# Gates ahead of attention, tap products on ScalarE, 2048-wide low parts and 54 fused pairs in a hybrid encoder layer

## The chip, the core and the metric

The kernel runs on one core of a Trainium2 chip. TensorE (PE in the profile) multiplies matrices into PSUM, VectorE (DVE) and ScalarE (ACT) work element by element, GpSimd (POOL) and SyncE (SP) issue DMAs here. Each engine works through its own instructions in the order in which the program issued them and waits on semaphores where an operand or a buffer isn't ready. The metric is the time of one execution on the device in microseconds, the median of several.

## What is computed

One mixer layer on x of 256 rows by 4096 columns:

```python
xn = rms_norm(x, norm_g[l])
h = jnp.einsum('bsd,de->bse', xn, w_in[l])            # 4096 x 14336
c_val, c_glu, c_gate, q, k, v, a_gate = jnp.split(h, split_pts, axis=-1)
conv_out = conformer_conv(c_val, c_glu, ...)          # GLU, 31 taps, LayerNorm, swish
conv_out = conv_out * jax.nn.silu(c_gate)
q = rms_norm(q..., q_norm_g[l]); k = rms_norm(k..., k_norm_g[l])
attn = longnet_mixture(q, k, v, rel_bias)             # 16 heads of 128
attn_out = attn * jax.nn.silu(a_gate)
mixed = jnp.concatenate([conv_out, attn_out], axis=-1)
x = x + jnp.einsum('bse,ed->bsd', mixed, w_out[l])    # 4096 x 4096
```

Everything is float32. The two large products read 302 MB of weights once.

## The kernel before

**Groups and pairs.** The output columns of both products are cut into 18 groups of 1024 (`GROUPS`, L46 to L52): 14 for `w_in` (four "conv", then "agv" and "qk" four times in turn, then two "gate"), and four "out" for `w_out`. Within a group the 4096 rows of the weights come as 16 pairs of two 128-row blocks, one pair being one DMA of 1 MB into a `raw` tile (L216, three buffers, on SP's queue). `ORDERS` (L58) gives the order of the pairs in an out group; a place in it is called a slot here.

**Splitting.** Each float32 operand is split into a high part that PE reads in one pass (`fp32r`) and a low part, the difference. A product is then three matmuls: high by high, low by high, high by low (`triple`, L895). For the weights ScalarE casts the high part (L830, L860, L875) and DVE subtracts (L831, L861, L876). A plain pair has 24 matmuls of 512 columns (2 blocks of k, 2 column halves e, 2 row halves s, 3 products).

**Fused pairs.** 40 of the 288 pairs (`FUSED`, L57) are multiplied as 2 x 2 blocks with seven products in place of eight (Winograd's form of Strassen's scheme): 21 matmuls. For that the weights' blocks need sums: `split_fused` (L848) has four steps. `one` splits blocks b11 and b21 and adds two sums over them (L869), `two` splits b22 (L876), `three` splits t1 and t3 (t13h, t13l) and makes two more sums (L883, L884), `four` splits t2 and t4 (t24h, t24l). Every sum is written over the raw tile, and the cast in the next step reads it. The sums on the side of x or of the mixer's output are made once (`block_sums`, L288).

**Buffers and the order of work.** The program issues matmuls slot by slot; ahead of each triple `before` (L901) issues as many steps of the splits as have room. Room is counted in tiles of 1024 columns: 8 (`ws`) and in groups from the first fused one on 4 more out of the pool `c4` (`W_MORE`). Steps come off one queue (`todo`) strictly in the order of the pairs, and DVE and ScalarE run them in that order. What else there is to do (the convolution's taps, normalisations, attention heads, splits of the mixer's output) are generators in lanes; `pump` (L666) advances them between matmuls as far as a budget allows: each engine gets `FILL` times the matmuls' nominal 227 ns, and every step books a planned cost.

**What lies around it.** The conv taps run on DVE, one per channel block (L447, 480 instructions). The conv tile is turned channel-first with DVE transposes and 64 ScalarE copies (L418); gates, q, k and the probabilities go through DRAM on POOL's queue for this (L360). Heads run only behind group 6 (`state["side"]`, L566), when PSUM's second half is free of fused sums. The two gate groups are the last input groups; their turned tiles wait for LayerNorm (L512), and the mixer's output is split (L631) before the out groups may read it.

Of the kernel before, what the change touches and what calls it, by code (L numbers as in the profile page):

```python
# [17 lines left out]
P = 128  # L18
# [17 lines left out]
FILL, SAVED = (0.93, 0.93), (700, 700)  # L36
# [3 lines left out]
C4 = 18  # L40
# [25 lines left out]
def _relative():  # L66
# [20 lines left out]
    return bucket, pattern  # L87

# [30 lines left out]
def layer_kernel(  # L119
# [12 lines left out]

    const = ctx.enter_context(tc.tile_pool(name="const", bufs=1))
# [12 lines left out]
    def side(name):  # L146
        return ps.tile([P, 512], F32, tag="side", bufs=4, name=name)
# [4 lines left out]
    def rsqrt(src, shape, mul, eps, name):  # L152

        n = int(np.prod(shape[1:]))
        tag = "rs_small" if n <= 32 else "rs_big"
        v = sb.tile(shape, F32, tag=tag, bufs=6, name=name + "v")
        r = sb.tile(shape, F32, tag=tag, bufs=6, name=name + "r")
        t = sb.tile(shape, F32, tag=tag, bufs=6, name=name + "t")
# [12 lines left out]
        return r  # L171
# [33 lines left out]
    def load_pair(j, cuts=(0, 2048), between=None):  # L205

# [54 lines left out]
    def split_xn(k):  # L261
# [12 lines left out]
        if k % 2 and k // 2 in FUSED[FUSED_IN[0]]:  # L274
            yield from block_sums(k // 2, src_of=xT, parts=(xh, xl), out=xsum, name="xs")

    split_gens = []
# [40 lines left out]
    state = {"side": False}  # L318

# [36 lines left out]

    aT, cT, mixA = {}, {}, {}
    conv_ready = {}

    def through_dram(ways, n, name):  # L360


        ds = []
        for i, (src, _) in enumerate(ways):
            ds.append(tc.dram_tile([P, 4 * n], F32, name=f"{name}d{i}"))
            nc.gpsimd.dma_start(ds[i], src)
        yield from landing()
        for d, (_, dst) in zip(ds, ways):
            for b in range(4):
# [7 lines left out]
                )  # L377
        yield from landing()

    def turn_far(tiles, name):  # L380
# [3 lines left out]
        ways = []  # L384
        for i, tile_ in enumerate(tiles):
            tmp = t4(f"{name}{i}").rearrange("p a b -> p (a b)")
            src = tile_.rearrange("p a b -> p (a b)")
            view = tmp.rearrange("p (b t s i) -> p s t b i", b=4, t=4, s=2)
            for s in range(2):
                nc.vector.transpose(  # L390
                    view[:, s],
                    src[:, 512 * s : 512 * s + 512].rearrange("p (t b x) -> p t b x", t=4, b=4),
                )
                yield 700
            ways.append((tmp, src))
        yield from through_dram(ways, 256, name)

    def turned(tile_):

        flat = tile_.rearrange("p a b -> p (a b)")  # L400
        v = flat.rearrange("p (a t s i) -> p t s a i", a=4, t=4, s=2)
        return [v[:, t] for t in range(4)]

    def turn(tile_, name):


        tmp = t4(name)
        src = tile_.rearrange("p a b -> p (a b)")
        flat = tmp.rearrange("p a b -> p (a b)")
        for s in range(2):  # L410
            nc.vector.transpose(flat[:, 512 * s : 512 * s + 512], src[:, 512 * s : 512 * s + 512])
            yield 700
        blocks = flat.rearrange("p (s t b x) -> p s t b x", s=2, t=4, b=4)
        dst = src.rearrange("p (t s a x) -> p s t a x", t=4, s=2, a=4)
        for b in range(4):
            for a in range(4):
                v = blocks[32 * a : 32 * a + 32, :, :, b, :]
                nc.scalar.copy(dst[32 * b : 32 * b + 32, :, :, a, :], v)  # L418
            yield 0, 1610

    def glu_post(cb, a):
        yield
        yield from turn(a, f"turn_a{cb}")
        aT[cb] = a
        conv_ready[cb] = True

    def conv_gen(cb):
        while cb not in conv_ready:
            yield
        a = aT[cb]  # L430
        c = cT[cb] = t4(f"cT{cb}")
        for tp in range(0, 4, 2):
            for t in (tp, tp + 1):
                ch = 4 * cb + t
                nc.vector.tensor_scalar(
                    c[:, t, :], a[:, t, :], wT[:, ch, MID : MID + 1], col("conv_b", ch),
                    op0=ALU.mult, op1=ALU.add,
                )
                yield 410
            for k in range(TAPS):  # L440
                sh = k - MID
                if sh == 0:
                    continue
                lo, hi = max(0, -sh), min(S, S - sh)
                for t in (tp, tp + 1):
                    ch = 4 * cb + t
                    nc.vector.scalar_tensor_tensor(  # L447
                        c[:, t, lo:hi], a[:, t, lo + sh : hi + sh], wT[:, ch, k : k + 1],
                        c[:, t, lo:hi], op0=ALU.mult, op1=ALU.add,
                    )  # L450
                    yield 470

# [3 lines left out]
    def channel_mean(srcs, name, tot=None):  # L456
# [12 lines left out]
        yield  # L469
        pm = side(name + "pm")  # L470
# [4 lines left out]
    conv_done = {}  # L475

    def ln_gen():
        pm = yield from channel_mean([cT[cb] for cb in range(4)], "mu")
        mu = sb.tile([P, S], F32, tag="rs_big", bufs=6, name="mu")
# [15 lines left out]
        for cb in range(4):  # L495
# [9 lines left out]
            conv_done[cb] = True  # L505

    mix_ready = {}

    def gate_post(cb, g):
        yield  # L510
        yield from turn_far([g], f"turn_g{cb}")
        while cb not in conv_done:  # L512
            yield
        for t in range(4):
            c = by_block(cT[cb][:, t, :])
            nc.vector.tensor_mul(c, c, turned(g)[t])
            mix_ready[NH + 4 * cb + t] = c
            yield 415
# [9 lines left out]
    def qk_norm(hg):  # L528
        st = sb.tile([P, 16], F32, tag="rs_small", bufs=6, name=f"ssqk{hg}")
        both = (qt[hg], kt[hg])  # L530
        for i, src in enumerate(both):
            v = src.rearrange("p a b -> p (a b)")
            for n in range(8):
                junk = sb.tile([P, DH], F32, tag="junk", bufs=2, name=f"sq{hg}_{i}_{n}")
# [7 lines left out]
        for i, src in enumerate(both):  # L542
# [9 lines left out]
        near = t4(f"near_q{hg}")  # L552
        far = qt[hg].rearrange("p a b -> p (a b)")
        nc.scalar.activation(
            near.rearrange("p t (s a i) -> p (t s) a i", s=2, a=4),
            far.rearrange("p (a t s i) -> p (t s) a i", a=4, t=4, s=2),
            AF.Copy, scale=gqk,
        )
        qt[hg] = near
# [3 lines left out]
    def head_gen(hg, hh):  # L563
        h = 4 * hg + hh
        hs = slice(DH * hh, DH * hh + DH)
        while hg not in qk_ready or not state["side"]:  # L566
            yield
        T = sb.tile([P, 384], F32, tag="toep", bufs=3, name=f"T{h}")
# [8 lines left out]
        yield from landing()  # L577
        psc = side(f"psc{h}").rearrange("p (i j) -> p i j", i=2)
# [583 lines left out]
```

## Time and profile before

| | |
|---|---|
| median of 3 runs | 1593.95 us (1593.34 to 1594.03) |
| the profiled execution | 1593.31 us, of which the span is 1591.5 us |
| plain / fused pairs | 248 / 40 |
| ScalarE casts of plain high parts (L830) | 511.4 us, 1050 ns each |
| DVE plain low parts (L831) | 598.3 us, 1221 ns each |
| DVE conv taps (L447) | 202.8 us, 469 ns each |
| DMA | 353 MB, mean 222 GB/s |

The span runs from the first to the last instruction; the execution's own time is 1.8 us longer. The profile counts an engine as busy while an instruction is in work. Matmuls are pipelined, so that PE looks busy for 389 ns per matmul while one starts every 227 ns; the count of matmuls in a stretch is the measure of its pace. A row of a timeline gives start, duration, engine, line, operation and operands, and in brackets how long the engine had been idle and what ended the wait. DVE instructions of one row with "x2" run one into the other, so that two take less than twice one.

### The profile page before, as it was taken

To read this page: it belongs to the slowest core of one execution; us is meant where nothing else is said; L and a number is where in the kernel's file an instruction comes from. 1 tells how busy PE (TensorE), PEld (TensorE's weight loads), DVE (VectorE), ACT (ScalarE), POOL (GpSimd) and SP (SyncE) were. 2 spreads that over 40 slices of the span, in tenths; PEclk is the share of its full clock that TensorE was granted. 3 is DMA by queue.
4 is the path that set the end of the run, shared out by engine and by line. 5 is a ranking of instruction groups with operands and counts; after the bars stand their busy time and mean duration, and the time that the engine had idled before them with its cause. 6 is when DMAs were issued, how large, how long until landed. Compare 5 with 4: busy or idle time off the path is not lost.

```text
span 1591.5 us, 19107 instructions
## 1 busy us (share of the span) xinstructions
PE 1580.2 (99%) x6946; PEld 1303.2 (82%) x6946; DVE 1271.8 (80%) x1752; ACT 859.4 (54%) x1250; POOL 88.2 (6%) x164
## 2 busy tenths in 40 slices
PE   9999999999999999999999999999999999999999
PEld 8888878888888888888888888888878888888887
DVE  6669888888889888788877887887767677888887
ACT  6765555464644563546453646356576544544453
POOL 0000000000000001111121010101030200000000
PEclk9999999999999999999999999999999999999999
DMA  9867454564756366576766575755765856466653
GB/s 380 290 207 272 171 226 185 196 228 159 262 187 238 134 262 211 203 233 218 253 211 224 200 253 185 245 207 212 234 219 196 265 207 254 187 237 238 233 213 136
DMA packets 63182, 353.05 MB, mean 222 GB/s; under 512 B 8784, under 2 KB 11600, under 8 KB 26480
## 3 DMA queue, kind: packets, MB, share of 16 engines
q1 hardware_dynamic: 54096, 326.38, 56.7%
q0 software_dynamic: 8704, 25.18, 5.4%
q8 instruction: 54, 0.88, 0.2%
q10 hardware_dynamic: 288, 0.28, 0.1%
q14 instruction: 40, 0.33, 0.1%
HBM read 334.99 MB, written 16.81 MB: 221 GB/s over the span
## 4 chain that ended last, share of the span: by engine, by line
PE 86%; DVE 8%; ACT 3%; issue 2%; DMA 1%; ACTq 0%; DVEq 0%
PE acc L775 16%; PE acc L776 16%; PE acc L778 16%; PE c L898 11%; PE c L897 10%; PE c L896 10%; DVE wl L831 2%; PE m L898 1%; PE m L897 1%; PE m L896 1%; DVE t13l L861 1%; DVE raw L869 1%; DVE bl L861 1%; ACT t24h L860 1%; ACT t13h L860 1%
## 5 line engine op out<-in xcount | busy, mean ns | idle before, releaser
L831 DVE TENSOR_TENSOR wl<-raw,wh 128x1024 fp32r<-128x1024 f32 x495 | 598.3, 1221 | 214.2 <-ACT wh L830 213.4
L830 ACT CAST wh<-raw 128x1024 fp32r<-128x1024 f32 x495 | 511.4, 1050 | 379.8 <-PE acc L776 204.6
L775 PE MATMUL acc<-wh,nh 128*128 128x512 f32 x896 | 355.1, 396 | 3.9 <-ACT wh L830 3.8
L776 PE MATMUL acc<-wh,nl 128*128 128x512 f32 x896 | 349.1, 390 | 0.0
L778 PE MATMUL acc<-wl,nh 128*128 128x512 f32 x896 | 242.0, 389 | 0.0
L447 DVE SCALAR_TENSOR_TENSOR cT<-conv,wT,cT 128x241 f32<-128x241 f32 (+14 forms) x480 | 202.8, 469 | 0.0
L775 PEld LDWEIGHTS acc<-wh,nh 128*128 128x128 f32 x896 | 168.3, 188 | 40.8 <-ACT wh L830 6.0
L778 PEld LDWEIGHTS acc<-wl,nh 128*128 128x128 f32 x896 | 168.2, 188 | 35.4
L776 PEld LDWEIGHTS acc<-wh,nl 128*128 128x128 f32 x896 | 168.2, 188 | 34.9
L897 PE MATMUL c<-wh,nl 128*128 128x512 f32 x480 | 186.7, 389 | 0.0
L898 PE MATMUL c<-wl,nh 128*128 128x512 f32 x480 | 186.7, 389 | 0.0
L896 PE MATMUL c<-wh,nh 128*128 128x512 f32 x480 | 186.7, 389 | 0.0
L898 PE MATMUL c<-wl,mh 128*128 128x512 f32 x352 | 137.3, 390 | 0.1
L896 PE MATMUL c<-wh,mh 128*128 128x512 f32 x352 | 137.2, 390 | 0.0
L897 PE MATMUL c<-wh,ml 128*128 128x512 f32 x352 | 137.0, 389 | 0.0
L897 PEld LDWEIGHTS c<-wh,nl 128*128 128x128 f32 x480 | 90.1, 188 | 18.8
L896 PEld LDWEIGHTS c<-wh,nh 128*128 128x128 f32 x480 | 90.1, 188 | 18.8
L898 PEld LDWEIGHTS c<-wl,nh 128*128 128x128 f32 x480 | 90.1, 188 | 18.5
L860 ACT CAST t24h<-raw 128x1024 fp32r<-128x1024 f32 x40 | 42.0, 1050 | 112.0 <-DVE raw L884 112.0
L775 PE MATMUL acc<-wh,xh 128*128 128x512 f32 x256 | 99.8, 390 | 0.0
L776 PE MATMUL acc<-wh,xl 128*128 128x512 f32 x256 | 99.7, 390 | 0.0
L860 ACT CAST t13h<-raw 128x1024 fp32r<-128x1024 f32 x40 | 42.1, 1051 | 105.1 <-DVE raw L869 102.4
(313 smaller groups left out, 1903.6 us busy)
## 6 DMA issues: line engine op xcount, KB each, us to landing
raw<-in_w_dram SPq DMA_DIRECT2D x286, 1024.0 KB, 4.9
xT<-in_x_cols_dram SPq DMA_DIRECT2D x15, 512.0 KB, 6.7
x<-in_x_dram SPq DMA_DIRECT2D x8, 512.0 KB, 8.4
xr<-in_x_dram SPq DMA_DIRECT2D x8, 512.0 KB, 6.3
out_dram<-xr SPq DMA_DIRECT2D x15, 256.0 KB, 7.2
T<-bias_dram SPq DMA_DIRECT2D x16, 192.0 KB, 5.0
raw<-in_w_dram SPq DMA_DIRECT2D x3, 512.0 KB, 6.1
turn_qk0d<-turn_qk POOLq DMA_DIRECT2D x2, 512.0 KB, 3.6
```

The lines of the kernel that those rows point to most:

```text
L447: nc.vector.scalar_tensor_tensor(c[:, t, lo:hi], a[:, t, lo + sh : hi + sh], wT[:, ch, k : k + 1], c[:, t, lo:hi], op0=ALU.mult, op1=ALU.add,)
L775: nc.tensor.matmul(a, hs, wp, start=k == 0, stop=False)
L776: nc.tensor.matmul(a, ls, wp, start=False, stop=False)
L778: nc.tensor.matmul(a, hs, wp, start=False, stop=k == KT - 1)
L830: nc.scalar.copy(h, src)
L831: nc.vector.tensor_sub(l, src, h.bitcast(F32))
L860: nc.scalar.copy(h, src)
L861: nc.vector.tensor_sub(l, src, h.bitcast(F32))
L869: nc.vector.tensor_add(r[:, 0:2, :], r[:, 0:2, :], r[:, 1:4:2, :])
L896: nc.tensor.matmul(acc, a[0], b[0], start=start, stop=False)
L897: nc.tensor.matmul(acc, a[1], b[0], start=False, stop=False)
L898: nc.tensor.matmul(acc, a[0], b[1], start=False, stop=stop)
```

## The change

- Order: the two gate groups come directly after the four conv groups; q and k ahead of gate and v in each head group. Gates and conv tiles are turned on DVE, stored in DRAM on POOL's queue and fetched when they are needed (`to_dram`, `from_dram`); the 64 ScalarE copies go.
- Taps: in groups with fused pairs a tap's products over four channel blocks run on ScalarE into one tile `cp`, and DVE adds it in one 1024-wide instruction; in groups without, DVE may also run a tap as before (`conv_products`, `conv_gen`).
- Splits: from the third group on a plain pair has one high and one low tile of 2048 columns; the low part is one subtraction. `ws` is 4 tiles of 2048. The 4 extra tiles of `c4` hold only parts of fused pairs, from two slots ahead of the group's first fused pair. PE runs a plain pair's matmuls with the high part first, then those with the low part.
- Fused pairs: five (slots 2, 4, 6, 8, 10) in six input groups, three in the first out group (slots 12 to 14) and seven in the other three: slots 2, 4, 6, 7, 9, 10 and 12. That makes 54. The blocks of fused weights are laid out in another order by the host; the b22 split now comes ahead of the first sums, which are one wide instruction in step `two`.
- All groups from the third on run through `Stream.group`; evacuation of groups without fused pairs is on ScalarE alone. The planner's `FILL` for DVE is 0.96 in place of 0.93, lanes are cut otherwise.

```diff
-FILL, SAVED = (0.93, 0.93), (700, 700)
+FILL, SAVED = (0.96, 0.93), (700, 700)
-C4 = 18
+C4 = 17
+GROUPS += [("gate", gp, C_GATE + 1024 * gp, C_GATE + 1024 * gp + 512) for gp in range(2)]
 for _hg in range(4):
+    GROUPS.append(("qk", _hg, C_Q + 512 * _hg, C_K + 512 * _hg))
     GROUPS.append(("agv", _hg, C_AG + 512 * _hg, C_V + 512 * _hg))
-    GROUPS.append(("qk", _hg, C_Q + 512 * _hg, C_K + 512 * _hg))
-GROUPS += [("gate", gp, C_GATE + 1024 * gp, C_GATE + 1024 * gp + 512) for gp in range(2)]
...
-FUSED_IN = range(2, 7)
-FUSED = [(2, 4, 6, 8) if g in FUSED_IN else () for g in range(N_IN)] + [range(2)] + 3 * [range(6)]
+FUSED_IN = range(2, 8)
+FUSED = [(2, 4, 6, 8, 10) if g in FUSED_IN else () for g in range(N_IN)]
+FUSED += [range(3)] + 3 * [range(7)]
-ORDERS += [(8, 9, 10, 11, 6, 7, 2, 3, 0, 12, 1, 13, 14, 4, 5, 15)]
-ORDERS += 3 * [(8, 9, 0, 10, 1, 11, 2, 6, 3, 7, 4, 12, 5, 13, 14, 15)]
-W_SLOTS, W_MORE = 8, 4
+ORDERS += [(3, 4, 5, 8, 9, 10, 11, 12, 13, 14, 15, 6, 0, 1, 2, 7)]
+ORDERS += 3 * [(8, 9, 0, 10, 1, 11, 2, 3, 12, 4, 5, 13, 6, 14, 15, 7)]
+W_SLOTS, W_MORE = 4, 4
...
+    def conv_products(cb):
...
+                nc.scalar.activation(
+                    cp[:, t, lo:hi], a[:, t, lo + sh : hi + sh], AF.Copy,
+                    scale=wT[:, 4 * cb + t, k : k + 1],
+                )
+                if t == 3:
+                    made.append((k, now[0] + 1500))
...
+            if made and made[0][1] <= now[0]:
...
+                nc.vector.tensor_add(c[:, :, lo:hi], c[:, :, lo:hi], cp[:, :, lo:hi])
...
+        def room(self, n, more):
+            held = self.held
+            return held["ws"] + n <= W_SLOTS and held["c4"] + more <= self.more
...
+        def split_plain(self, u):
+            def high():
+                h = self.tile(f"wh{u}", (u, "h"), "ws")
+                for k in range(2):
+                    nc.scalar.copy(h[:, 1024 * k : 1024 * k + 1024], raw_tiles[u][:, k])
...
+            def low():
+                h, l = self.parts[(u, "h")], self.tile(f"wl{u}", (u, "l"), "ws")
+                src = raw_tiles[u].rearrange("p k c -> p (k c)")
+                nc.vector.tensor_sub(l, src, h.bitcast(F32))
...
+            return [(ONE, high), (ONE, low)]
...
             def one():
-                r = blocks()
-                both("b", r[:, 0:3:2, :], ("b11", "b21"))
-                nc.vector.tensor_add(r[:, 0:2, :], r[:, 0:2, :], r[:, 1:4:2, :])
+                both("b", blocks()[:, 0:2, :], ("b11", "b21"))
             def two():
                 r = blocks()
...
+                nc.scalar.copy(h, r[:, 2, :])
+                nc.vector.tensor_sub(l, r[:, 2, :], h.bitcast(F32))
+                nc.vector.tensor_add(r[:, 0:4:3, :], r[:, 0:3:2, :], twice(r[:, 3, :]))
             def three():
+                both("t13", blocks()[:, 0:4:3, :], ("t1", "t3"))
                 r = blocks()
+                nc.vector.tensor_add(r[:, 2, :], r[:, 0, :], r[:, 2, :])
+                nc.vector.tensor_add(r[:, 1, :], r[:, 2, :], r[:, 1, :])
             def four():
-                both("t24", blocks()[:, 0:2, :], ("t2", "t4"))
+                both("t42", blocks()[:, 1:3, :], ("t4", "t2"))
...
+                self.more = W_MORE if firsts and slot + 2 >= firsts[0] else 0
...
+            for part in "hl":
                 for e in range(2):
                     self.before()
+                    for k, (a, b) in enumerate(self.blocks_of(u, j, rows, part)):
...
+                del self.parts[(u, part)]
+                self.free((u, part))
+            pump()
```

More of the change, by code (lines that the diff above doesn't have):

```diff
@@ L274, in split_xn, with run @@
         if k % 2 and k // 2 in FUSED[FUSED_IN[0]]:
-            yield from block_sums(k // 2, src_of=xT, parts=(xh, xl), out=xsum, name="xs")
-    split_gens = []
+            sums = block_sums(k // 2, src_of=xT, parts=(xh, xl), out=xsum, name="xs")
+            if k < KT // 2:
+                yield from sums
+            else:
+                late_sums.append(sums)
+    split_gens, late_sums = [], deque()
+    def run(gen):
+        for cost in gen:
+            spend(*(cost if isinstance(cost, tuple) else (cost or 0,)))
     def split_more():
@@ L402, in turned @@
         return [v[:, t] for t in range(4)]
[L404 to L419, printed above, removed]
+    a_dram = {}
@@ L815, in step @@
         def step(self):
[L817 removed]
+            if not self.todo or not any(self.room(*need) for need in self.todo[0][0]):
                 return False
@@ new lines, in plain, with plain_last @@
+                    credit((8 if part == "h" else 4) * PRODUCT)
+                    if part == "h":
+                        pump()
+                del self.parts[(u, part)]
+                self.free((u, part))
+            pump()
+        def plain_last(self, u, j, rows, s, e, one):
+            acc = one[f"c{s + 1}{e + 1}"]
+            for part in "hl":
+                for k, (a, b) in enumerate(self.blocks_of(u, j, rows, part)):
+                    end = part == "l" and k == 1
+                    nc.tensor.matmul(acc, a[s][0], b[e], start=False, stop=end)
+                    if part == "h":
+                        nc.tensor.matmul(acc, a[s][1], b[e], start=False, stop=False)
+            credit(6 * PRODUCT)
```

397 lines of the change are left out of this document (242 added, 155 removed).

## The prediction

> **What bounds the kernel now.** I read the busy shares, then the matmul count over a long stretch, then stretches of one column group each, then the waits of PE, then the timelines of DVE and PE through one out group.
>
> ```profile
> span 1591.5 us, 19107 instructions
> PE 1580.2 (99%) x6946; PEld 1303.2 (82%) x6946; DVE 1271.8 (80%) x1752; ACT 859.4 (54%) x1250; POOL 88.2 (6%) x164
> PE 86%; DVE 8%; ACT 3%; issue 2%; DMA 1%; ACTq 0%; DVEq 0%
> 300.00:1100.00 800.00, 800.00 (x3531) 1.00 0.62 215
> 180.20:264.50 84.30, 82.43 (x358) 66.59 (x357) 72.76 (x91) 47.21 (x63) 0.00 (x0) 1.00 0.56 210
> 200.00:230.00 30.00, 28.70 (x124) 1.00 0.48 180
> 264.50:348.80 84.30, 84.30 (x374) 69.82 (x373) 72.64 (x93) 46.51 (x60) 0.00 (x0) 1.00 0.53 196
> 1163.00:1249.40 86.40, 82.47 (x358) 66.65 (x357) 61.76 (x107) 59.60 (x99) 16.44 (x30) 1.00 0.71 233
> PE m L898 <- DVE t24l L861: 2.3, 6, 0.5
> PE acc L775 <- ACT wh L830: 3.8, 4, 1.4
> ```
>
> From 300 to 1100 us PE never pauses: 800/3531 = 0.2266 us per matmul, at granted clock 1.00. All 6946 at that pace are 1573.7 us, so 17.8 us of the span is loss. It sits at the ends of the run, in the first fused group (358 matmuls where the next one has 374; between 200 and 230 us 124 where 30/0.2266 + 2 = 134 would stand, 2.2 us), in the last input group (1163 to 1249: 358 where 86.4/0.2266 = 381 would fit, 5.2 us) and in short waits for t24l. A plain pair is 24 matmuls, 5.44 us; a fused pair 21, 4.76 us. PE is the bound on average; the chain's 8% of DVE says that somewhere DVE takes over. That place is the fused stretch. One cycle of an out group, a fused pair and a plain pair on DVE (columns: start, duration, engine, line):
>
> ```profile
> 1433.57 1.22 DVE L861 TENSOR_TENSOR bl<-raw,bh 128x1024 fp32r<-128x1024 f32 x1
> 1434.82 1.22 DVE L869 TENSOR_TENSOR raw<-raw 128x1024 f32<-128x1024 f32 x1
> 1435.97 0.69 DVE L876 TENSOR_TENSOR b22s<-raw,b22s 128x512 fp32r<-128x512 f32 x1
> 1437.24 1.23 DVE L861 TENSOR_TENSOR t13l<-raw,t13h 128x1024 fp32r<-128x1024 f32 x1 [0.59 <-ACT t13h L860]
> 1438.50 0.69 DVE L883 TENSOR_TENSOR raw<-raw 128x512 f32<-128x512 f32 x1
> 1439.23 0.69 DVE L884 TENSOR_TENSOR raw<-raw 128x512 f32<-128x512 f32 x1
> 1441.09 1.23 DVE L861 TENSOR_TENSOR t24l<-raw,t24h 128x1024 fp32r<-128x1024 f32 x1 [1.17 <-ACT t24h L860]
> 1442.23 2.35 DVE L831 TENSOR_TENSOR wl<-raw,wh 128x1024 fp32r<-128x1024 f32 x2
> 1444.51 1.22 DVE L861 TENSOR_TENSOR bl<-raw,bh 128x1024 fp32r<-128x1024 f32 x1
> ...
> 1440.01 1.05 ACT L860 CAST t24h<-raw 128x1024 fp32r<-128x1024 f32 x1 [2.80 <-DVE raw L884]
> ```
>
> The fused pair holds DVE for 8.66 us (1433.57 to 1442.23), the plain pair for 2.28. Twice DVE waits for ScalarE, which itself waits for DVE's sum: a ping-pong, 0.59 and 1.17 us, that no buffer shortens. The cycle is 10.94 us, PE needs 10.20, so DVE falls back 0.74 us per cycle and lives on the lead it has when the group begins:
>
> ```profile
> 1419.91 0.39 PE L896 MATMUL c<-wh,mh 128*128 128x512 f32 x1
> 1430.16 1.23 DVE L861 TENSOR_TENSOR t24l<-raw,t24h 128x1024 fp32r<-128x1024 f32 x1 [1.17 <-ACT t24h L860]
> 1430.79 0.39 PE L896 MATMUL m<-bh,mh 128*128 128x512 f32 x1
> 1434.64 0.39 PE L898 MATMUL m<-t24l,msp 128*128 128x512 f32 x1
> 1486.18 0.50 PE L898 MATMUL m<-t24l,msp 128*128 128x512 f32 x1 [0.36 <-DVE t24l L861]
> ```
>
> Call the group's start T0 (1419.91). Its first t24l is ready at T0+11.48 and read at T0+14.73: lead 3.25 us. Five cycles cost 3.7, and the sixth t24l is late by some 0.5, which PE shows. The arithmetic closes: six alternating fused pairs are the most that this order carries.
>
> **The change, part by part.**
>
> *Matmuls.* 14 more fused pairs save 3 each: 42 x 0.2266 = 9.5 us. Six input groups of 5 fused pairs take 83.6 us of PE, three out groups of 7 take 82.3.
>
> *The fused pair's DVE order.* The new order is b low, b22 low, wide sum, t13 low, two sums, t42 low. The b22 low, which covered half the wait for t13h, now stands ahead of the sum that t13h waits for. From the rows above: b low 1.15, b22 low 0.6, sum and then the whole wait 1.23+1.17, t13 low 1.15, sums 0.73+0.69+1.17, t42 low 1.14: 9.05 us in place of 8.66. A cycle is then 11.33 against 10.20, and in the out groups fused pairs stand back to back (2,3 and 4,5): there DVE needs 9.05 for PE's 4.76.
>
> *Low parts 2048 wide, four slots.* One subtraction replaces two. The two take 2.35 us together, being pipelined; one of twice the length I put at 2.28, the start-to-start time of the two (1442.23 to 1444.51), between 2.26 (twice the 1.13 that the second adds) and 2.44 (twice 1.22). What changes is the lead: four slots of 2048 hold this plain pair and the next, and only fused parts may use the extra tiles. Today 12 slots of 1024 hold the next two pairs at a group's end. So slot 1's high part starts at T0, takes 2 x 1.0 on ScalarE, its low part follows at T0+2.2, the first fused pair at T0+4.45, and t42 low ends at T0+13.6. Read at T0+14.73: lead 1.15 instead of 3.25.
>
> [...]
>
> *Out groups (three).* After the first fused pair come six fused and four plain pairs to the last: DVE 6 x 9.05 + 4 x 2.28 = 63.4, PE 6 x 4.76 + 4 x 5.44 = 50.3. Lost: 13.1 - 1.15 = 11.9 us each, 35.7 in all. A check without leads, with the sums of L1014 to L1021 and four output sums of 2.5 (first and last of eight):
>
> ```profile
> 1409.23 0.68 DVE L1014 TENSOR_TENSOR xr<-xr,m 128x512 f32<-128x512 f32 x1
> 1413.55 0.68 DVE L1021 TENSOR_TENSOR xr<-xr,vs 128x512 f32<-128x512 f32 x1
> 1419.83 2.47 DVE L686 TENSOR_TENSOR xr<-xr,c 128x512 f32<-128x512 f32 x4
> ```
>
> 7 x 9.05 + 9 x 2.28 + 4.9 + 2.5 = 91.3 of DVE in 82.3 of PE: at least 9.0 us per group whatever the lead, 27 in all.
>
> *First out group.* Three fused pairs in a row at slots 12 to 14. The extra tiles open at slot 10, so the first t42 low is 3.4 us early; the next two cost 9.05 - 4.76 = 4.29 each: 8.6 - 3.4 = 5.2 us.
>
> *Input groups (six).* Four cycles after the first fused pair lose 4 x 1.13 = 4.5, a lead of up to 1.15 helps, sums (a fifth block sum of xn among them) and tap adds that fall outside DVE's waits hurt. I take 4.5 each, 27 us. Bounds: nothing, if the tap adds fill the waits and the lead is regained; 9 us, if none does: 5 x 9.05 + 11 x 2.28 + 5 for the group's own sums + 15 for other work = 90 against 83.6, and 2.5 for its start.
>
> *Taps, conv turn, gates.*
>
> ```profile
> L447 DVE SCALAR_TENSOR_TENSOR cT<-conv,wT,cT 128x243 f32<-128x243 f32 x32 | 14.5, 465 | 0.0
> L869 DVE TENSOR_TENSOR raw<-raw 128x1024 f32<-128x1024 f32 x40 | 49.0, 1225 | 1.4
> L254 ACT ACTIVATE xh<-xT,first_x 128x256 fp32r<-128x256 f32 x31 | 15.5, 499 | 0.2 <-DMA xT<-in_x_cols_dram 0.2
> L418 ACT COPY conv<-turn_a 32x256 f32<-32x256 f32 x64 | 25.8, 403 | 0.8
> turn_qk0d<-turn_qk POOLq DMA_DIRECT2D x2, 512.0 KB, 3.6
> T<-bias_dram SPq DMA_DIRECT2D x16, 192.0 KB, 5.0
> ```
>
> A tap on four channel blocks is 4 x 0.465 = 1.86 us of DVE; as a product it is 4 x 0.5 = 2.0 of ScalarE and one add of 1.23. At most 120 taps: 76 us of DVE less, 240 of ScalarE more, which has 46% of the span free. This relief falls in groups where DVE has room anyway; the plain groups and the out groups gain no PE time by it. A DVE add that waits for its product is queued ahead of the next low part; the product must have been issued 1.5 us before, so I cost it inside the input groups' range. 64 turn copies (25.8 us) leave ScalarE; for each conv block POOL issues one store and four loads, beside weights on SP's queue at a DMA share of 0.53 to 0.56. Nobody waits who isn't given 8.5 us: nothing, or up to 3 us if weights land late. The 16 loads of T go out on SP earlier, between weight loads; they are small and land in 5.0 us: nothing. The gates run before attention, so normalisation, last heads and mix splits no longer crowd the last input group; of its 5.2 us I leave 1 (between 0 and 5.2, as heads still end there).
>
> *Sum.* 6904 x 0.2266 = 1564.3. Old loss 17.8, less 4.2 at the last input group, less 5.2 of old fused waits (2.2 in the first fused group, some 0.75 in each of four out groups) that the new terms replace: 8.4. New: 27 + 5.2 + 35.7 = 67.9. Span 1640.6. The profiled execution took 1593.31 for its span of 1591.5, and the median is 0.64 above that: 1643.
>
> **Rivals.**
>
> *PE stays the bound.* DVE and ScalarE keep pace, and the fewer matmuls count: 1564.3 + 8.4 + 3 for small waits + 2.4 = 1578. For it: 20% of DVE is idle, and its waits could hold other work. It decides at the fused pair's DVE period: below (82.3 - 20.5 - 7.4)/7 = 7.8 us an out group is PE's. Against it: the row of 1441.09, and nothing else is left to do in the out groups. [...]
>
> *Only the out groups fall back.* In the input groups tap adds sit in the waits and the lead is kept: 1643 - 27 = 1616. For it: those groups ran at 374 matmuls per 84.3 us on a cycle of 10.9. Against it: fewer slots, and a fifth fused pair.
>
> *The input groups are full.* ScalarE's products delay casts, and each loses 9: 1643 + 27 = 1670.
>
> **How the numbers follow.** Forecast 1643 (1622 to 1660): 0.60. Out groups only, 1603 to 1622: 0.17. Input groups full, above 1660: 0.08. PE-bound, 1578: 0.12. Terms that cancel, within 0.2%, which is about what a measurement of this kernel can tell from no change: 0.03. The range 1603 to 1668 leaves out the last two and the upper half of the full case, 0.19. Faster 0.12, same 0.03, slower 0.85.
>
> **What would show it.** 6904 matmuls; in out groups a fused pair every 9.0 us on DVE where two stand together, waits of about 1.2 before both t13l and t42l, PE waiting for t42l some 11 to 12 us per group; DVE's share of the chain well above 8%; out groups of 91 to 94 us and fused input groups of 86 to 90. I am wrong if t13l doesn't wait, if an out group takes under 85 us, or if the fused input groups hold 83.6.

## The result, and the profile after

The kernel after took **1694.07 us** (median of 4 runs, 1692.72 to 1695.4) against 1593.99 for before on the same chip: a ratio of 1.0629, 95% interval 1.061 to 1.0647. The forecast was 1643 with a range up to 1668. The direction and the mechanism (DVE and ScalarE wait for each other in the fused groups) are as predicted. The size is not: the time lies 26 us above the range.

The page of the profile after: span, busy time, and the shares of the chain that ended last.

```profile
span 1693.6 us, 18693 instructions
PE 1613.2 (95%) x6904; PEld 1296.9 (77%) x6904; DVE 1280.0 (76%) x1414; ACT 977.2 (58%) x1525; POOL 99.0 (6%) x184
PE 52%; DVE 24%; ACT 14%; issue 9%; DMA 1%; ACTq 0%; DVEq 0%
```

The matmuls fell to 6904 as forecast, DVE is hardly busier than before (1280.0 us against 1271.8), and yet the chain runs over DVE, ScalarE and issue for 47% of the span. No engine is full: the 6904 matmuls at 0.2266 us each need 92% of the span. Engines wait for each other. Of the 76 us for which the profile shows PE waiting, 69 stand at the t parts of fused pairs (line that waits, releaser, us in total, times, longest):

```profile
PE m L1036 <- ACT t L1001: 41.6, 44, 2.7
PE m L1038 <- DVE t L1002: 27.6, 55, 0.5
```

Two stretches by windows (length, then for each engine busy time and instructions, granted clock, DMA share, GB/s): the fused input group that starts at 368.8 us, and an out group.

```profile
368.80:461.00 92.20, 87.42 (x370) 69.73 (x369) 71.95 (x64) 51.78 (x72) 0.53 (x1) 0.98 0.53 189
1496.70:1593.20 96.50, 89.12 (x365) 69.37 (x364) 74.23 (x70) 42.84 (x48) 0.00 (x0) 0.96 0.54 196
```

A group's **loss** is from here on its length, from its first matmul to the next group's, less 0.2266 us for each of its pairs' matmuls (369 for a fused input group, 363 for an out group with seven fused pairs): 92.2 - 83.6 = 8.6 and 96.5 - 82.2 = 14.3. Groups are counted from 0; 2 to 7 are the fused input groups, 14 is the first out group, 15 to 17 are the others. A loss in a group in which heads run, 14 among them, also holds the heads' matmuls, which are work and no pause. Losses in us:

| kernel | span | 2 | 3 | 4 | 5 | 6 | 7 | 14 | 15 | 16 | 17 |
|---|---|---|---|---|---|---|---|---|---|---|---|
| before | 1591.5 | 3.5 | 0.0 | 0.0 | 0.0 | 0.1 | plain | 1.4 | 0.7 | 1.0 | 1.0 |
| after | 1693.6 | 12.9 | 8.3 | 8.6 | 11.4 | 12.0 | 11.7 | 10.7 | 16.8 | 14.3 | 14.4 |
| e1_split_low | 1660.7 | 10.3 | 5.8 | 6.1 | 7.5 | 8.1 | 9.8 | 10.0 | 13.9 | 10.8 | 11.1 |
| e2_sum_first | 1665.8 | 10.6 | 5.9 | 6.2 | 9.1 | 8.1 | 9.3 | 9.1 | 13.8 | 10.9 | 11.1 |
| e3_interleaved | 1598.1 | 8.6 | 0.1 | 0.0 | 1.6 | 2.2 | 2.5 | 6.7 | 3.4 | 2.9 | 2.8 |
| e4_no_products | 1700.8 | 12.9 | 5.8 | 5.8 | 7.9 | 7.9 | 9.9 | 40.4 | 17.1 | 14.2 | 14.4 |
| e5_40_pairs | 1643.6 | 9.8 | 6.5 | 6.6 | 8.1 | 8.2 | plain | 4.9 | 8.5 | 7.7 | 7.9 |
| e6_before_seven | 1611.4 | 3.5 | 0.0 | 0.0 | 0.0 | 0.1 | plain | 1.4 | 7.7 | 8.6 | 7.9 |
| e7_five_slots | 1674.5 | 14.4 | 8.9 | 7.6 | 6.9 | 7.1 | 11.5 | 8.9 | 16.6 | 13.2 | 13.3 |
| e11_first_four | 1585.2 | 5.9 | 0.0 | 0.0 | 1.6 | 1.3 | 2.1 | 4.7 | 0.0 | 0.0 | 0.2 |

At 0.2266 us the 6904 matmuls are 1564.3 us, so that 129.3 us of the span are loss, where the forecast had 76.3: the fused input groups 64.9 (forecast 27), group 14 7.1 (5.2) without the 3.6 us of head matmuls in its 10.7, the other out groups 45.5 (35.7), all else 11.8 (8.4). Of the miss of 53.0 us, 49.6 stand in the fused groups.

The same stretch of DVE that was shown of before, now of after: from the low part of one t42 to the next pair's, in the out group that starts at 1397.7 us (start, duration, engine, line, operation, operands, and in brackets the wait and its releaser).

```profile
1437.19 1.22 DVE L1002 TENSOR_TENSOR b<-raw,b 128x1024 fp32r<-128x1024 f32 x1
1438.33 0.69 DVE L1015 TENSOR_TENSOR b<-raw,b 128x512 fp32r<-128x512 f32 x1
1438.93 1.22 DVE L1016 TENSOR_TENSOR raw<-raw 128x1024 f32<-128x1024 f32 x1
1441.31 1.23 DVE L1002 TENSOR_TENSOR t<-raw,t 128x1024 fp32r<-128x1024 f32 x1 [1.17 <-ACT t L1001]
...
1444.97 1.23 DVE L1002 TENSOR_TENSOR t<-raw,t 128x1024 fp32r<-128x1024 f32 x1 [1.11 <-ACT t L1001]
1446.87 2.29 DVE L984 TENSOR_TENSOR wl<-raw,wh 128x2048 fp32r<-128x2048 f32 x1 [0.67 <-ACT wh L977]
1449.08 1.22 DVE L1002 TENSOR_TENSOR b<-raw,b 128x1024 fp32r<-128x1024 f32 x1
...
1458.04 1.22 DVE L1002 TENSOR_TENSOR b<-raw,b 128x1024 fp32r<-128x1024 f32 x1
```

The fused pair that is followed by another takes 8.96 us (1449.08 to 1458.04; forecast 9.05), with waits of 1.1 to 1.2 before both t parts, as forecast. But a **third wait** of 0.67 us stands before the plain pair's low part. ScalarE shows why (same stretch of after):

```profile
1443.90 1.04 ACT L1001 CAST t<-raw 128x1024 fp32r<-128x1024 f32 x1 [2.62 <-DVE raw L1024]
1444.85 1.99 ACT L977 CAST wh<-raw 128x1024 fp32r<-128x1024 f32 x2
```

The plain pair's two casts start right behind the cast of t42's high part and end at 1446.84. The 2048-wide subtraction needs both, so it can't start when DVE is done with t42 at 1446.20. The first of two halves needs only the first cast, which ends some 0.9 us earlier (1.99 us for the two casts, 1.04 for one); before had no such wait (1442.23, shown with the prediction). A cycle of a fused and a plain pair is therefore 1437.19 to 1449.08, 11.9 us, and 12.0 in an input group (307.43 to 319.43), where the forecast had 11.33 and the matmuls need 10.20.

In the input groups the third wait varies: in the cycles of group 3 it is between nothing and 1.45 us. ScalarE and DVE of after in group 3:

```profile
302.42 0.88 ACT L484 ACTIVATE cp<-a,wT 128x244 f32<-128x244 f32 x2
303.21 1.98 ACT L977 CAST wh<-raw 128x1024 fp32r<-128x1024 f32 x2
```

```profile
305.22 2.29 DVE L984 TENSOR_TENSOR wl<-raw,wh 128x2048 fp32r<-128x2048 f32 x1 [1.45 <-ACT wh L977]
307.43 1.22 DVE L1002 TENSOR_TENSOR b<-raw,b 128x1024 fp32r<-128x1024 f32 x1
```

Two tap products stand ahead of the casts here, and the wait is 1.45 us.

### The profile page after: what moved, and what is told of

Its sections match the earlier page's. It is cut to its first block, busy times and chain, and to the rows that moved or that the text cites. A ratio compares the mean times of both kernels' runs of the same rounds, so it can differ in the third digit from the quotient of the medians.

```text
span 1693.6 us, 18693 instructions
## 1 busy us (share of the span) xinstructions
PE 1613.2 (95%) x6904; PEld 1296.9 (77%) x6904; DVE 1280.0 (76%) x1414; ACT 977.2 (58%) x1525; POOL 99.0 (6%) x184
## 4 chain that ended last, share of the span: by engine, by line
PE 52%; DVE 24%; ACT 14%; issue 9%; DMA 1%; ACTq 0%; DVEq 0%
PE c L1147 24%; PE c L1149 12%; ACT wh L977 7%; ACT t L1001 5%; DVE t L1002 5%; DVE b L1002 4%; PE acc L885 3%; PE acc L886 3%; PE acc L888 3%; DVE wl L984 3%; DVE raw L1016 3%; PE c L1162 2%; DVE raw L1024 2%; DVE raw L1023 2%; DVE b L1015 2%
## 5 line engine op out<-in xcount | busy, mean ns | idle before, releaser
L984 DVE TENSOR_TENSOR wl<-raw,wh 128x2048 fp32r<-128x2048 f32 x202 | 461.9, 2289 | 188.4 <-ACT wh L977 187.1
L1147 PE MATMUL c<-wh,nh 128*128 128x512 f32 x1200 | 471.7, 393 | 4.0 <-ACT wh L977 3.8
L1149 PE MATMUL c<-wh,nl 128*128 128x512 f32 x1200 | 469.9, 392 | 0.0
L1001 ACT CAST t<-raw 128x1024 fp32r<-128x1024 f32 x108 | 113.2, 1048 | 336.0 <-DVE raw L1016 186.1
L1147 PE MATMUL c<-wl,nh 128*128 128x512 f32 x1200 | 299.6, 392 | 0.0
L1147 PEld LDWEIGHTS c<-wh,nh 128*128 128x128 f32 x1200 | 227.9, 190 | 54.9 <-ACT wh L977 6.5
L1149 PEld LDWEIGHTS c<-wh,nl 128*128 128x128 f32 x1200 | 227.3, 189 | 47.7
L1147 PEld LDWEIGHTS c<-wl,nh 128*128 128x128 f32 x1200 | 225.2, 188 | 47.0 <-DVE wl L984 0.3
L1002 DVE TENSOR_TENSOR t<-raw,t 128x1024 fp32r<-128x1024 f32 x108 | 132.3, 1225 | 126.0 <-ACT t L1001 126.0
L484 ACT ACTIVATE cp<-a,wT 128x241 f32<-128x241 f32 (+13 forms) x288 | 125.1, 491 | 108.7 <-DVE cT L515 108.6
```

Source lines behind the costliest of these rows:

```text
L484: nc.scalar.activation(cp[:, t, lo:hi], a[:, t, lo + sh : hi + sh], AF.Copy, scale=wT[:, 4 * cb + t, k : k + 1],)
L984: nc.vector.tensor_sub(l, src, h.bitcast(F32))
L1001: nc.scalar.copy(h, src)
L1002: nc.vector.tensor_sub(l, src, h.bitcast(F32))
L1147: nc.tensor.matmul(acc, a[s][0], b[e], start=begin, stop=False)
L1149: nc.tensor.matmul(acc, a[s][1], b[e], start=False, stop=False)
```

## The experiments

Three theories. **P**: the order within the pairs is the cause; DVE and ScalarE wait for each other three times per cycle, and the third wait is the wide low part's. **B**: four wide slots hold the streams back. **T**: the tap products on ScalarE and their adds are the cause. A fourth, **C**, came with the second set: the 14 further pairs are the cause, whatever the code of a pair. All kernels but the tenth to the twelfth have one time each, beside a before of 1593.5 us (1593.93 for the seventh).

**1. The low part in two halves again** (all else as after).

```diff
-                nc.vector.tensor_sub(l, src, h.bitcast(F32))
+                for c in (slice(0, 1024), slice(1024, 2048)):
+                    nc.vector.tensor_sub(l[:, c], src[:, c], h[:, c].bitcast(F32))
```

> The low part of a plain pair is made in two subtractions of 1024 columns, the first needing only the first cast. Theory P (DVE and ScalarE wait for each other within each fused pair and at the plain low part behind it; the sum of these waits sets the fused stretches): the wait of 0.67 us before the plain low part goes, the cycle of a fused and a plain pair falls from 12.0 to 11.3 us, 36 such cycles lie behind a group's first fused pair, and the first fused pair of nine groups starts up to 0.9 us earlier: 24 to 32 us less, 1662 to 1670. Theory B (four wide slots: the lead is lost to a lack of buffers): the buffers are the same, 1694 within 4. Theory T (tap products on ScalarE and their adds): untouched, 1694 within 4.

Measured 1662.58 us, 31.5 less than after, inside P's range. DVE of this kernel, one cycle in an out group:

```profile
1412.60 1.22 DVE L1003 TENSOR_TENSOR b<-raw,b 128x1024 fp32r<-128x1024 f32 x1
...
1420.39 1.23 DVE L1003 TENSOR_TENSOR t<-raw,t 128x1024 fp32r<-128x1024 f32 x1 [1.11 <-ACT t L1002]
1421.53 2.35 DVE L985 TENSOR_TENSOR wl<-raw,wh 128x1024 fp32r<-128x1024 f32 x2
1423.80 1.22 DVE L1003 TENSOR_TENSOR b<-raw,b 128x1024 fp32r<-128x1024 f32 x1
```

The third wait is gone, the cycle is 11.20 us, and the two halves take 2.35 us where one wide subtraction takes 2.29: the wide form saved 0.06 us of work and cost 0.67 of waiting. With 36 cycles behind the first fused pairs that is some 24 of the 31.5 us (36 x 0.67, an estimate); the rest fits the earlier start that the expectation names, and wasn't told apart.

**2. The wide sum ahead of the b22 low part**, as before's order had it.

```diff
-                nc.vector.tensor_sub(l, r[:, 2, :], h.bitcast(F32))
                 nc.vector.tensor_add(r[:, 0:4:3, :], r[:, 0:3:2, :], twice(r[:, 3, :]))
+                nc.vector.tensor_sub(l, r[:, 2, :], h.bitcast(F32))
```

> In the fused pair the wide sum is issued ahead of the b22 low part, as before the change. Theory P: the b22 low part covers 0.57 us of the wait for t13h, the fused pair on DVE falls from 8.96 to 8.4 us; some 53 fused pairs: 26 to 32 us less, 1662 to 1668. Theories B and T: 1694 within 4.

Measured 1667.57 us, 26.5 less, inside P's range. DVE of this kernel at the t13 low part:

```profile
1419.22 1.23 DVE L1015 TENSOR_TENSOR raw<-raw 128x1024 f32<-128x1024 f32 x1
1420.36 0.69 DVE L1016 TENSOR_TENSOR b<-raw,b 128x512 fp32r<-128x512 f32 x1
1421.62 1.23 DVE L1002 TENSOR_TENSOR t<-raw,t 128x1024 fp32r<-128x1024 f32 x1 [0.57 <-ACT t L1001]
```

The b22 low part fills half the wait for t13's high part: 0.57 in place of 1.17. The two edits, neither with a matmul more or less, move 31.5 and 26.5 us; the two together, without the third edit, were not run.

**3. Both, and the last step of a fused pair issued behind the next plain pair's two steps** (or behind the next fused pair's first step), so that DVE has a low part to make while ScalarE casts t42. Loads are counted by a running number, since steps of two pairs now cross. A PSUM slot that the planner lends out is returned one slot earlier.

```diff
+                steps = [(n, f, u) for n, f in make(u)]
+                late = self.todo.pop() if self.todo and self.todo[-1][3:] else None
+                if late:
+                    cut = 2 if len(steps) == 2 else 1
+                    steps.insert(cut, late[:3])
+                self.todo.extend(steps)
+                if ORDERS[g][slot] in FUSED[g]:
+                    self.todo.append(self.todo.pop() + ("late",))
...
-            if not self.todo or self.todo[0][2] != u:
+            self.left[u] -= 1
+            if not self.left[u]:
                 del raw_tiles[u]
-                load_pair(u + RAW)
+                load_pair(self.next_load)
+                self.next_load += 1
```

> Both edits above, and the last step of a fused pair is issued behind the next plain pair's two steps, or behind the first step of a fused one, so that the waits hold other work (weight loads then go out in the order of the pairs; heads use PSUM's second half one slot less per group). Theory P: a fused and a plain pair take DVE some 9.5 us, less than PE's 10.2, two fused pairs and a plain one 16.7 against 15.0; fused input groups come to 84 to 86 us, out groups to 83 to 86: 1580 to 1600. Theory B: the slots are as few, 1650 or more. Theory T: out groups recover some 45 us, fused input groups keep most of their loss: 1630 to 1650.

Measured 1600.05 us, 94.0 less than after and 0.05 beyond P's upper end; B and T, which forecast 1630 and more, fall as the main cause. DVE of this kernel:

```profile
1512.42 1.22 DVE L1017 TENSOR_TENSOR b<-raw,b 128x1024 fp32r<-128x1024 f32 x1
...
1516.10 1.23 DVE L1017 TENSOR_TENSOR t<-raw,t 128x1024 fp32r<-128x1024 f32 x1 [0.60 <-ACT t L1016]
...
1518.63 2.36 DVE L999 TENSOR_TENSOR wl<-raw,wh 128x1024 fp32r<-128x1024 f32 x2
1521.48 1.23 DVE L1017 TENSOR_TENSOR t<-raw,t 128x1024 fp32r<-128x1024 f32 x1 [0.48 <-ACT t L1016]
1522.62 1.22 DVE L1017 TENSOR_TENSOR b<-raw,b 128x1024 fp32r<-128x1024 f32 x1
```

ScalarE ahead of the second t:

```profile
1520.39 1.06 ACT L1016 CAST t<-raw 128x1024 fp32r<-128x1024 f32 x1 [2.43 <-PE c L1162]
```

The plain pair's low parts (1518.63) stand where the wait for t42's high part was, with four wide slots and all tap products still there. A cycle is 10.20 us, exactly what the matmuls need, and that is now PE's pace: the cast at 1520.39 waited 2.43 us for PE, and DVE's wait of 0.48 us hangs on it. Where DVE has to catch up, in group 15 of this kernel, a cycle takes it 9.54 us, the 9.5 that P expected. The interleaving was not run alone; what is left beside the first two edits, 94.0 - 31.5 - 26.5 = 36 us, is its share if the three add up.

**4. No tap products in groups with fused pairs**; all taps run in the plain groups.

```diff
-        if left[1] > 800:
+        if left[1] > 800 and state["taps"]:
```

> In groups with fused pairs no tap products run on ScalarE and none are added; all taps run in groups without. Theory P: the fused stretches keep their cycle of 12.0 us and lose only the adds and the casts' delay behind products: 4 us less in each of six groups, some 24 us: 1665 to 1680, more if the convolution then ends late. Theory T: the fused input groups come down to 84 us, 60 us less: 1630 to 1640. Theory B: 1690 or more.

Measured 1702.57 us. As a total that is far from T, above P's 1665 to 1680 (P allowed for more if the convolution ends late) and within B's open "1690 or more", so that the total doesn't tell P from B. The groups say more. The fused input groups lose 50.2 us in place of 64.9: the products and their adds cost 14.7 there. But the convolution is then late, and in the first out group PE waits for the split of its output (waits of PE in this kernel):

```profile
PE c L1147 <- ACT mh L750: 18.5, 5, 6.2
```

Group 14 loses 40.4 in place of 10.7. So the products do cost something, and pay it back with more.

**5. The kernel after with before's 40 pairs and out orders.**

```diff
-FUSED_IN = range(2, 8)
-FUSED = [(2, 4, 6, 8, 10) if g in FUSED_IN else () for g in range(N_IN)]
-FUSED += [range(3)] + 3 * [range(7)]
+FUSED_IN = range(2, 7)
+FUSED = [(2, 4, 6, 8) if g in FUSED_IN else () for g in range(N_IN)]
+FUSED += [range(2)] + 3 * [range(6)]
```

> The kernel after with before's 40 fused pairs and before's orders of the out groups; the wide adds, tap products and 2048-wide low parts stay. Theory P (each cycle of a fused and a plain pair takes VectorE 12.0 us instead of 10.94, whatever the number of pairs, because it waits three times for ScalarE): an out group loses six times 12.0 - 10.2 less a lead of 1.2, some 9 to 10 us, five input groups lose 8 to 10 each, the extra matmuls cost 9.5: 1655 to 1672. Rival C (the 14 further pairs are the cause, and the new code of a pair is harmless): 1594 to 1605. B (four wide slots) 1655 to 1694.

Measured 1645.42 us, below P's range and B's, and far above C's. With before's number of pairs the rest of the change still costs 52 us. P counted six cycles between six fused pairs where there are five, which is some 5 us of what its range lies too high; its input groups were put at 8 to 10 us and lost 6.5 to 9.8. DVE of this kernel, between the t42 low part of one pair and the b low part of the next:

```profile
1462.43 1.22 DVE L1002 TENSOR_TENSOR b<-raw,b 128x1024 fp32r<-128x1024 f32 x1
...
1472.20 2.29 DVE L984 TENSOR_TENSOR wl<-raw,wh 128x2048 fp32r<-128x2048 f32 x1 [0.67 <-ACT wh L977]
1474.41 1.22 DVE L1002 TENSOR_TENSOR b<-raw,b 128x1024 fp32r<-128x1024 f32 x1
```

Five cycles of 11.98 against 10.20 and a lead of 1.15 give 7.8; measured 8.5, 7.7 and 7.9.

**6. The kernel before with seven fused pairs in the last three out groups**, in the order of after (`range(7)` for `range(6)`, and after's order).

> The kernel before with seven fused pairs in place of six in the last three out groups, in the order of the kernel after; nothing else. Theory P: VectorE's 8.66 us of a fused pair against 4.8 us of matmuls; the lead of 3.25 us is used up where two fused pairs follow each other, and each of the three groups loses 5 to 10 us, less 0.7 for three matmuls: 1607 to 1622. Rival C in its strong form (back-to-back fused pairs alone make the out groups of the kernel after slow): +13 to 15 each, 1633 to 1640. That before had room for them: 1591 to 1594.

Measured 1613.24 us: inside P's range, 19.7 us slower than before. DVE of this kernel, two fused pairs in a row:

```profile
1458.85 1.23 DVE L861 TENSOR_TENSOR t24l<-raw,t24h 128x1024 fp32r<-128x1024 f32 x1 [1.19 <-ACT t24h L860]
...
1467.46 1.23 DVE L861 TENSOR_TENSOR t24l<-raw,t24h 128x1024 fp32r<-128x1024 f32 x1 [1.19 <-ACT t24h L860]
```

8.61 us from one t24 low part to the next, where PE needs 4.76. Before's own code had no room for a seventh pair in that order, with fused pairs side by side; a seventh pair apart from the others was not run in it. Of the 13 to 16 us that an out group of after loses beyond before's 0.7 to 1.0, about 7 come with the seventh pair and its order, and the rest with the rest of the change.

**7. Five wide slots in place of four** (`W_SLOTS` 5, paid for with two tiles of `c4`; in groups without fused pairs a lent PSUM slot is returned two slots earlier).

> The kernel after with five slots of 2048 for plain halves in place of four, paid for with two slots of 1024 (15 in place of 17). Theory P: the waits inside the pairs stay, only the lead at a group's start may grow, by one step of some 2.3 us for each fused group: 1672 to 1698. B (four slots hold the streams back): most of the loss goes, 1600 to 1650.

Measured 1676.27 us, 17.8 less: inside P's range, though the slots that B names are worth up to these 18 us. DVE's waits ahead of the plain low part, first in after, then the longest three in this kernel:

```profile
DVE wl L984 <- ACT wh L977: 187.1, 122, 8.1
```

```profile
DVE wl L984 <- ACT wh L977: 38.2, 48, 2.2
DVE wl L984 <- PE c L1149: 30.4, 24, 3.2
DVE wl L984 <- ACT cp L484: 18.4, 18, 2.2
```

The row of after's largest wait falls by 149 us, but much of that has only moved to other releasers: over all of them DVE waits 188 us ahead of the plain low part in after and 131 here. These 57 us bring 18, since 113 of after's 187 stand in groups 8 to 13, which have no fused pairs and where PE waits only 5 us in all. The waits for t, inside the fused pairs, stay (126.0 us in after, 127.4 here). Half of the gain stands in groups 5 and 6, which lose 11.4 and 12.0 us in after and 6.9 and 7.1 here; why those two was not followed.

**8 to 12. Versions that are faster than after, and some a little faster than before.** In the third kernel two fused pairs side by side and a plain one still take DVE 16.8 to 17.1 us where the matmuls need 15.0; this is what the next kernels avoid. The eighth kernel is the third with before's counts and orders in the out groups (2, 6, 6, 6; 50 pairs in all).

> The interleaved kernel with before's counts and orders in the four out groups (2, 6, 6, 6 fused pairs, alternating with plain ones), 50 fused pairs in all. Theory P: with a cycle of 10.2 us on VectorE against 10.2 of matmuls the out groups lose 0.5 to 1.5 us each in place of 2.9 and 3.4, and the first of them 2 to 4 in place of 6.7: 1591 to 1597. B (slots): out groups lose as before, 1600 to 1604.

Measured 1590.76 us, 0.2 below the expected range. Groups 15 to 17 lose 0.0, 0.0 and 0.2, group 14 3.5.

The ninth also makes two block sums of x later in the first fused group.

```diff
-                if late_sums and slot % 2:
+                if late_sums and slot in (5, 7):
```

> As the kernel with 50 interleaved pairs, and the block sums of x for the fused pairs 8 and 10 of the first fused group are made behind slots 5 and 7 in place of 1 and 3. Theory: they delay that group's second t42 high part (4.5 us of its 8.6 us loss); moved, the group loses 3 to 5 us: 3 to 5 us below the kernel with 50 interleaved pairs, 1586 to 1593. Rival: they only move the stall to where they stand now: no change, or up to 4 us slower.

Measured 1589.82 us, 0.9 below the eighth: the expected 3 to 5 did not come, and group 2 loses 8.2 in place of 8.8. Moving the sums did not remove that loss.

The tenth has seven fused pairs in the last three out groups, with a plain pair after each (53 pairs).

> The kernel with 50 interleaved pairs and later block sums, with seven fused pairs in place of six in each of the last three out groups, no two of them adjacent (53 in all). Theory P: a fused and a plain pair take VectorE no longer than TensorE (10.2 us), so the groups still lose nothing and each is shorter by three matmuls (0.68 us): 2 us below the kernel with 50, 1586.5 to 1589. Rival (no lead left for a seventh: as with two adjacent fused pairs): each group loses 2 to 3 us, 1592 to 1597.

Measured 1592.14 us (median of 11 runs, 1590.37 to 1596.22; ratio to before 0.9991, interval 0.9982 to 1.0001): a miss for P, in the rival's range. Groups 15 to 17 lose 0.0, 1.8 and 1.9. DVE and PE of this kernel in group 16, which starts at 1419.5:

```profile
1426.15 1.22 DVE L1017 TENSOR_TENSOR b<-raw,b 128x1024 fp32r<-128x1024 f32 x1
...
1435.69 1.22 DVE L1017 TENSOR_TENSOR b<-raw,b 128x1024 fp32r<-128x1024 f32 x1
```

```profile
1435.83 0.50 PE L1053 MATMUL m<-t,msp 128*128 128x512 f32 x1 [1.41 <-DVE t L1017]
```

The loss is not a lack of room within the group. Group 15 carries its seven pairs without loss; in group 16 a cycle takes DVE 9.54 us, and PE waits once, for the first fused pair. That pair's first b low part comes 6.7 us after the group's start, against 3.2 in group 15. Ahead of it on DVE stand the output sums of group 15's last fused pair, which now lies in the last slot but one. So, by the trace, the seventh pair costs the next group its early start; an order of seven that ends earlier was not run.

The eleventh is the ninth with four fused pairs (4, 6, 8, 10) in the first fused group, 49 in all; two other lines follow from it (which block sums of x are made early, and when a lent PSUM slot is returned in groups without fused pairs). The twelfth is the ninth again.

```diff
+FUSED[2] = (4, 6, 8, 10)
```

> The kernel with 50 interleaved pairs and later block sums, with four fused pairs (slots 4, 6, 8, 10) in place of five in the first fused group, 49 in all. The first group loses 8.2 us, 4.5 of it in waits for fused pairs at 197 to 237 us, where VectorE is busy nearly throughout. Theory P: two plain pairs more ahead of the first fused one give VectorE 6 us of lead, the group loses 3 to 5 us less and pays 0.68 for three matmuls: 1585.5 to 1588 beside 1589.8. Rival (the lead is capped by the four slots, so that the fused pairs only wait later): 1589.5 to 1592.

> The kernel with 50 interleaved pairs and later block sums again, timed in rounds against before. From its single time of 1589.8: 1589 to 1592, a ratio of 0.997 to 0.999 with an interval below 1. Rival: the single time was lucky, 1592 to 1595 and an interval that holds 1, as with 53 pairs.

Measured **1587.28 us** for the eleventh (median of 5 runs; ratio to before 0.996, interval 0.9946 to 0.9973) and 1589.18 for the twelfth (of 6; 0.997, 0.9959 to 0.9982): both as expected, and 0.3 to 0.4% below before. Windows of the twelfth, then of the eleventh, around the first fused pair:

```profile
190.00:200.00 10.00, 7.21 (x28) 5.04 (x27) 9.33 (x10) 5.46 (x6) 0.00 (x0) 0.96 0.42 126
200.00:210.00 10.00, 10.00 (x40) 8.08 (x40) 8.41 (x10) 5.57 (x6) 0.00 (x0) 0.87 0.55 211
```

```profile
190.00:200.00 10.00, 10.00 (x46) 8.28 (x45) 9.93 (x12) 4.85 (x7) 0.56 (x1) 1.00 0.91 306
200.00:210.00 10.00, 8.75 (x38) 6.61 (x37) 8.95 (x10) 7.31 (x12) 0.00 (x0) 1.00 0.40 142
1419.90:1503.00 83.10, 83.10 (x368) 68.81 (x367) 71.35 (x75) 41.64 (x45) 0.00 (x0) 1.00 0.64 229
```

With the first fused pair two slots later PE waits less, group 2 loses 5.9 in place of 8.2, and PE runs through a stretch as long as an out group, most of it in group 16, without a pause (1419.9 to 1503.0). Group 16 itself, 366 matmuls, takes 83.0 us.

## Why the prediction was right, and where it failed

- **What bounds before: held.** With a seventh fused pair, in after's order, before's out groups lose 7.7 to 8.6 us each in place of 0.7 to 1.0.
- **Matmuls: held.** 6904, 9.5 us fewer.
- **The fused pair's DVE order: held.** 8.96 us back to back (9.05 forecast, whose terms as listed add up to 9.03), with waits of 1.17 and 1.11 where 1.17 twice was forecast. Turning the order back brought 26.5 us.
- **"Low parts 2048 wide, four slots": this is the step that failed.** It priced the wide subtraction right as work, 2.28 (measured 2.29), and then said "What changes is the lead". It did not ask what the wide instruction waits for. It needs both casts of ScalarE, which stand behind the cast of t42's high part, and waits 0.67 us in a cycle of an out group. The forecast put this wait at nothing. Splitting the instruction brought 31.5 us, some 24 of them by the wait itself: the largest single part of the 53 us that the forecast lacked.
- **The lead: held in the groups that start on time.** The first t42 low part was forecast to end 13.6 us after the group's start. PE and DVE of after in group 16:

```profile
1496.69 0.39 PE L1147 MATMUL c<-wh,mh 128*128 128x512 f32 x1
```

```profile
1508.55 1.23 DVE L1002 TENSOR_TENSOR t<-raw,t 128x1024 fp32r<-128x1024 f32 x1 [1.17 <-ACT t L1001]
```

  It ends 13.1 us after the start, and so does group 17's: a lead of 1.6 in place of 1.15. In group 15, which follows three fused pairs at the end of group 14, it ends after 15.6, 0.9 us late. By the forecast's own formula with the third wait in it, 6 x 8.96 + 4 x (2.29 + 0.67) = 65.6 on DVE against 50.3 on PE, less 1.6, is 13.7 (measured 14.3 and 14.4), and plus 0.9 is 16.2 (16.8).
- **Out groups: right in form, short by 2.4 to 4.9 us each**, by four third waits (2.7 us) and, in group 15, the late start.
- **First out group: 10.7 against 5.2.** Most of the difference is no wait. The heads' matmuls in its first 66 us:

```profile
L718 PE MATMUL po<-pr,agv 128*128 128x256 f32 x16 | 3.6, 379 | 0.0
```

  16 matmuls of a head, 3.6 us, run within it and are no loss, which leaves 7.1 against the forecast's 5.2. PE's waits run from 1379.35 us, behind its first fused pair, to 1389.64, at the last t42 low part; behind that, at the group's end, the granted clock was 0.53 from 1389.64 to 1392.60, with a matmul every 0.43 us (last section).
- **Input groups: the second term that failed, 64.9 us in all against 27.** 8.3 to 12.9 us each, against 4.5 and an upper bound of 9. Four cycles of 12.0, with the third wait in them, less the lead are 6.0; without tap products groups 3 and 4 lose 5.8. The products add 2.5 to 4.1 in groups 3 to 6 and 1.8 in group 7 and stand ahead of the casts, which is the sentence "I cost it inside the input groups' range" at work. Group 2 loses 12.9 with and without them. A later first fused pair is part of the remedy (in the interleaved kernel two plain pairs more ahead of it brought 2.3 us), and the rest of its loss stays open.
- **Taps, turn, gates at nothing: nearly held outside the fused groups.** All losses outside groups 2 to 7 and 14 to 17 come to 11.8 us, forecast 8.4. That the products carry the convolution along in time is a gain the forecast did not see: without them group 14 loses 40.4.
- **The rivals.** PE staying the bound (1578) and only the out groups falling back (1616) are refuted by the losses of all fused groups. "The input groups are full" (1670) was the nearest, with a chance of 0.08: ScalarE's products did delay casts, but the split low part alone brought 31.5 us and the products, taken out, 14.7 in these groups; no rival had the third wait.

## What to carry to other kernels

Where two engines feed each other in order, price a chain and not an engine: for each instruction of one cycle write down which part of the other engine's work it needs and when that ends, and add the waits to the cycle; together DVE and ScalarE were the bound of these out groups, though DVE was busy for 74 of 96.5 us and ScalarE for 43. Merging two instructions into one saved 0.06 us of work here and made the merged one wait for the last of its inputs. Put independent work of the next tile into each wait instead; order and splitting alone took 94 us out here, without any work removed. Then set the number and the places of the expensive tiles by the cycle: as long as DVE's is shorter than the matmuls', tiles that stand apart lost nothing within an out group here, while two side by side did, and one next to a group's end took the next group's lead.

## What was not expected of the hardware

In bursts within the stalled groups a matmul of after started every 0.43 us in place of 0.2266. Windows of after around one of them, in group 16:

```profile
1536.80:1543.20 6.40, 3.37 (x12) 1.67 (x11) 3.74 (x4) 3.78 (x4) 0.00 (x0) 1.00 0.19 76
1543.20:1546.70 3.50, 3.50 (x11) 2.72 (x10) 3.33 (x2) 1.61 (x3) 0.00 (x0) 0.53 0.81 283
```

After 6.4 us in which PE had 12 matmuls, the granted clock was 0.53 for 3.5 us, with a matmul every 0.43 us, and then 0.99 over the next 9.3 us. Single waits in that group were 1.3 us at most. What sets off a burst was not tested. About 67 matmuls of after, in ten such bursts, were slowed so, by 0.2 us each: some 13 us, and by estimate the span lost less than that, since PE would have waited for DVE soon after anyway. How much of the 129 us it is was not tested apart. The kernel of 1587.28 us, whose profile gives a granted clock of 1.00 over the run (after: 0.99), shows none.
